# A transformer stack on one core: w_out products behind the next chunk's gate products, norms in parts, modulation vectors on VectorE

## The chip, the cores and the metric

The kernel runs on one core of one Trainium2 chip. The metric is the device time of one execution in microseconds; lower is better. The engines are named as in the profile: PE (TensorE, matrix products), PEld (its weight loads), DVE (VectorE), ACT (ScalarE), POOL (GpSimd) and SP (SyncE, which issues the DMAs).

## The reference

Three blocks follow each other on 512 latent tokens of width 1024, with 256 context tokens beside them in the first layer. Layer 0 is an even mixer (window attention and a gated recurrence) with an FFN, layer 1 an odd mixer (retention) with an FFN, and then a second block (gated delta rule and dilated attention) follows. Each layer computes:

```python
m_lat = jnp.split((cond_lat @ mod_w[layer] + mod_b[layer])[:, None, :], 6, axis=-1)
m_ctx = jnp.split((cond_ctx @ mod_w[layer] + mod_b[layer])[None, None, :], 6, axis=-1)
...
x = x + m_lat[5] * swiglu(modulate(rms_norm(x, norm_g[layer, 1]), m_lat[3], m_lat[4]), ffn_w_in[layer], ffn_w_out[layer])
if not last:
    ctx = ctx + m_ctx[5] * swiglu(modulate(rms_norm(ctx, norm_g[layer, 1]), m_ctx[3], m_ctx[4]), ffn_w_in[layer], ffn_w_out[layer])
...
def swiglu(h, w_in, w_out):
    return (jax.nn.silu(gate) * up) @ w_out    # gate, up = the halves of h @ w_in
```

The FFN is 2816 wide. The second block starts with `mod = silu(c) @ ada_w + ada_b` (3072 columns) and a modulated norm of its own. All is in float32.

## The kernel before

Activations lie transposed: features on the 128 partitions (8 tiles, index k or m_), tokens along the row, 512 for the group `lat` (`xl`, normed copies `hH`, `hL`), 256 for the group `cx` (`xc`, `cH`, `cL`). Every float32 product is made of three PE passes over a high and a low part (`mm3`, lines 140 to 142): wH*xH, wH*xL, wL*xH. Weights come by DMA from SP as 1 MB tiles `wr`; ACT copies the high part `wh` and POOL subtracts the low part `wl` (`wcols`, `wsplit`).

An FFN (`ffn`) runs over 11 chunks of 256 hidden units. In a chunk PE makes, for each group and each half j of the chunk, 24 products for the gate and 24 for the up part; ACT makes the silu, VectorE multiplies (`sg`, line 381) and the result is split again into `aH` (ACT, line 152) and `aL` (VectorE, line 153). Then come the products with w_out, eight output tiles per group of six products each, and VectorE adds each to `xl` or `xc` (`residual`, line 358). The first FFN (f0) has both groups, the second (f1) only `lat`. The PSUM pool `mm` has seven banks there.

A norm (`norm`) sums the squares of the eight tiles (ACT squares into `nt`, VectorE adds into `nacc`, line 339), PE adds over the partitions with a matrix of ones (line 342), ACT makes the reciprocal root (lines 324, 325), and VectorE, ACT and POOL make `hH` and `hL` (lines 348 to 355). Both groups go through it together, and the products behind it start when it is through with the first tiles.

The modulation vectors are matvecs with weights `mod_w` and `ada_w`. They are generators in a list `self.bg`; `tick` advances the first by one 1 MB load. `matvec` multiplies on PE (line 247, tile `mv`), with the loads in side pools `mv1` (8 columns of tiles of layer 1, at the first FFN's norm and behind its end) and `mv2` (12 loads of the second block, around the second FFN). `matvec_dve` multiplies on VectorE (line 277, tile `macc`), and only the sums are handed to PE (line 283); it makes the other vectors of layer 1 in the first FFN.

The order on each engine is fixed when the program is built: a scheduler takes instructions by priority, mostly the order of the code, as their inputs are expected. On the chip each engine runs its list in order.

## Time and profile before

| | us |
|---|---|
| median of 3 runs | 3009.43 (3008.18 to 3015.25) |
| profiled execution | 3007.48 |
| its span, first to last instruction | 3005.4 |
| PE busy | 2810.6 (94%) |
| DVE, ACT, POOL busy | 1372.2, 1053.6, 986.4 |

The mean granted clock of PE over the span is 0.973 of full speed. Busy times of engines overlap, so that they don't add up to the span; where PE is busy, the other engines' work costs no time of its own. The windows of the section on rows cut the span where PE passes from one stage to the next.

### The profile page before, as it was taken

The page shows a single profiled execution, that of the slowest core. Times are in us where ns is not written, and L with a number is a line of the kernel's source. Part 1 is how long each engine was busy: PE and PEld are TensorE (multiplying, and loading weights), DVE is VectorE, ACT ScalarE, POOL GpSimd, SP SyncE. Part 2 cuts the span into 40 slices and gives each one's busy share as a digit, 9 for nine tenths or more (in the row PEclk, how much of TensorE's full clock was granted, in tenths as well). Part 3 has the DMA queues.
Part 4 walks back from the last instruction along what each step waited for, and adds up shares of the span by engine and source line. Part 5 has one row for each costly group of instructions (what it writes and reads, how often), then busy time and mean ns, then how long its engine had stood idle before and what let it go on. Part 6 is the DMA issues. An engine that isn't in the chain of part 4 may idle for free. (4 is left out here: it accounts for less than half of the span.)

```text
span 3005.4 us, 38050 instructions
## 1 busy us (share of the span) xinstructions
PE 2810.6 (94%) x15400; PEld 2288.8 (76%) x15400; DVE 1372.2 (46%) x2218; ACT 1053.6 (35%) x1920; POOL 986.4 (33%) x498
## 2 busy tenths in 40 slices
...
PEclk7999999999999999999999999999999999999999
...
GB/s 263 72 86 82 35 102 69 93 233 98 126 83 142 56 56 71 63 71 70 56 84 56 85 43 168 100 96 98 85 112 156 167 137 87 142 124 108 225 72 89
DMA packets 220824, 312.68 MB, mean 104 GB/s; under 512 B 27430, under 2 KB 172360, under 8 KB 214120
## 3 DMA queue, kind: packets, MB, share of 16 engines
...
## 5 line engine op out<-in xcount | busy, mean ns | idle before, releaser
L134 POOL TENSOR_TENSOR wl<-wr,wh 128x1024 fp32r<-128x1024 f32 x200 | 484.3, 2424 | 921.4 <-ACT wh L133 908.9
L140 PE MATMUL mm<-hH,wh 128*128 128x512 f32 x1760 | 705.8, 402 | 12.9 <-ACT hH L354 7.1
L141 PE MATMUL mm<-hL,wh 128*128 128x512 f32 x1760 | 704.4, 400 | 10.0 <-POOL hL L352 8.9
L142 PE MATMUL mm<-hH,wl 128*128 128x512 f32 x1760 | 700.6, 398 | 0.0
L133 ACT ACTIVATE wh<-wr 128x1024 fp32r<-128x1024 f32 x200 | 211.3, 1058 | 583.1 <-PE mm L141 461.7
L140 PEld LDWEIGHTS mm<-hH,wh 128*128 128x128 f32 x1760 | 334.4, 190 | 94.0 <-ACT hH L354 11.5
L120 POOL TENSOR_TENSOR wl<-wr,wh 128x1024 fp32r<-128x1024 f32 x96 | 236.5, 2466 | 510.1 <-ACT wh L119 484.3
L141 PEld LDWEIGHTS mm<-hL,wh 128*128 128x128 f32 x1760 | 334.2, 190 | 89.8 <-POOL hL L352 13.7
L142 PEld LDWEIGHTS mm<-hH,wl 128*128 128x128 f32 x1760 | 334.4, 190 | 72.8 <-issue 4.4
L358 DVE SCALAR_TENSOR_TENSOR xl<-mm,modT,xl 128x512 f32<-128x512 f32 x216 | 160.4, 749 | 152.1 <-PE mm L142 144.8
L141 PE MATMUL mm<-aL,wh 128*128 128x512 f32 (+1 forms) x528 | 194.9, 369 | 32.9 <-DVE aL L153 32.9
L381 DVE TENSOR_TENSOR sg<-mm,sg 128x512 f32<-128x512 f32 (+1 forms) x66 | 39.7, 601 | 405.0 <-PE mm L142 404.9
L140 PE MATMUL mm<-aH,wh 128*128 128x512 f32 (+1 forms) x528 | 191.1, 367 | 4.0 <-ACT aH L152 4.0
L142 PE MATMUL mm<-aH,wl 128*128 128x512 f32 (+1 forms) x528 | 191.0, 365 | 0.0
L141 PE MATMUL mm<-cL,wh 128*128 128x256 f32 x640 | 184.9, 289 | 0.9 <-POOL cL L352 0.9
L140 PE MATMUL mm<-cH,wh 128*128 128x256 f32 x640 | 183.9, 287 | 1.7 <-ACT rsg L914 1.7
L142 PE MATMUL mm<-cH,wl 128*128 128x256 f32 x640 | 183.7, 287 | 0.0
L119 ACT ACTIVATE wh<-wr 128x1024 fp32r<-128x1024 f32 x96 | 100.9, 1053 | 143.1 <-PE mm L141 83.3
L141 PEld LDWEIGHTS mm<-aL,wh 128*128 128x128 f32 x528 | 102.9, 195 | 55.2 <-DVE aL L153 39.7
L153 DVE TENSOR_TENSOR aL<-sg,aH 128x512 fp32r<-128x512 f32 (+1 forms) x66 | 111.9, 1695 | 44.4 <-ACT aH L152 44.4
L141 PEld LDWEIGHTS mm<-cL,wh 128*128 128x128 f32 x640 | 123.0, 192 | 8.0 <-issue 4.2
L140 PEld LDWEIGHTS mm<-cH,wh 128*128 128x128 f32 x640 | 123.2, 193 | 5.4 <-ACT rsg L914 2.2
...
## 6 DMA issues: line engine op xcount, KB each, us to landing
...
```

The costliest lines, as they stand in the source:

```text
L119: self.nc.scalar.activation(H, rv, AF.Copy)
L120: self.nc.gpsimd.tensor_tensor(L, rv, f32(H), ALU.subtract)
L133: self.nc.scalar.activation(H, v, AF.Copy)
L134: (engs[j] if engs else self.nc.gpsimd).tensor_tensor(L, v, f32(H), ALU.subtract)
L140: mm(out, lH, rH, start=first, stop=False, **kw)
L141: mm(out, lH, rL, start=False, stop=False, **kw)
L142: mm(out, lL, rH, start=False, stop=last, **kw)
L153: (eng or self.nc.gpsimd).tensor_tensor(L, src, f32(H), ALU.subtract)
L358: self.nc.vector.scalar_tensor_tensor(g.x[:, m_, :], po, gate[:, m_:m_ + 1], g.x[:, m_, :], ALU.mult, ALU.add)
L381: nc.vector.tensor_tensor(sg, pu, sg, ALU.mult)
```

## The change

Six things are changed together.

- **FFN in a pipeline.** In chunk c PE makes the gate products, then the w_out products of chunk c-1 (`down`), then the up products. The up weights are loaded apart, `sg` and `aH`/`aL` get buffers for that, and `mm` has eight banks.
- **Norms in parts.** `norm` works on a `Part`: a group, or half of `lat` (256 tokens). Ahead of the FFNs and the odd mixer only the first part is normed; the second part's norm is placed by `between` in the first products (`gemm2`, two weight tiles in turn), and its ones-matmul is put behind the product of k = 3 (`behind`). There `nt` of the first part and the sums `nr` lie in PSUM.
- **Matvecs.** The eight loads of `mod_w` that PE multiplied in layer 1 and the twelve of `ada_w` go to `matvec_dve`, three ticks in each of chunks 1 to 10 of the first FFN (two in chunks 0 to 8 before) and two in chunks 1 to 8 of the second.
- **Ends in parts.** The even mixer's output products run group by group; the odd mixer's last projection and the last w_out products of the second FFN run by halves of 256 tokens.
- **Second block.** Its norm runs by halves with `nt` in PSUM; the transposes of the tokens (`tokens_out`) are no longer deferred.
- The calls of `later`, which deferred ticks, are gone.

The core of the diff (`up` and `gate` are new functions inside `ffn`; `between` is `norm_of(parts[1], mod)`, which calls `norm` with the product to stay behind):

```diff
+    def gemm2(self, pss, ws, part, between=None):
+        for k in range(KT):
+            if between and k == 4:
+                between(last)
+            for ps, (wH, wL) in zip(pss, ws):
+                last = self.mm3(ps[:, part.c], wH[:, k, :], wL[:, k, :], *part.split(k), k == 0, k == KT - 1)
...
+    def matvec_dve(self, ps, sb, i0, n, m, w, c0, bias, dst, tag):
         nc = self.nc
-        m = 2048 // n
         nj = m // 512
+        per = 2048 // m
...
+        for k0 in range(0, KT, per):
+            r = self.wt("wr", [P, per, m])
+            for k in range(per):
                 for i in range(n):
-                    c = self.cond[:, k0 + k, i:i + 1]
+                    c = self.cond[:, k0 + k, i0 + i:i0 + i + 1]
...
+    def norm_stats(self, ps, part, tag="sm", pt=None, after=None):
+        nc, sb, m = self.nc, self.np, part.m
+        acc = self.T(sb, [P, CTX if part.i else LAT], f"nacc{part.i}")[:, :m]
         for k in range(KT):
-            for g, acc in zip(groups, accs):
-                if k == 0:
-                    nc.scalar.activation(acc, g.x[:, k, :], AF.Square)
-                else:
-                    sq = tmp(g)
-                    nc.scalar.activation(sq, g.x[:, k, :], AF.Square)
-                    nc.vector.tensor_tensor(acc, acc, sq, ALU.add)
-        for g, acc in zip(groups, accs):
-            pt = self.T(ps, [P, 512], tag)
-            nc.tensor.matmul(pt[:, :g.m], self.ones, acc, start=True, stop=True)
-            self.rstd(acc, pt[:, :g.m], 1.0 / D)
-        for g, acc, (A, S) in zip(groups, accs, mods):
-            for k in range(KT):
-                t = tmp(g)
-                H, L, s = g.H[:, k, :], g.L[:, k, :], S[:, k:k + 1]
-                nc.vector.scalar_tensor_tensor(t, g.x[:, k, :], A[:, k:k + 1], acc, ALU.mult, ALU.mult)
-                if k % 2:
-                    nc.scalar.activation(t, t, AF.Identity, bias=s)
-                    nc.scalar.activation(H, t, AF.Copy)
-                    nc.gpsimd.tensor_tensor(L, t, f32(H), ALU.subtract)
-                else:
-                    nc.scalar.activation(H, t, AF.Identity, bias=s)
-                    nc.vector.scalar_tensor_tensor(L, t, s, f32(H), ALU.add, ALU.subtract)
-
-    def residual(self, g, m_, po, gate):
-        self.nc.vector.scalar_tensor_tensor(g.x[:, m_, :], po, gate[:, m_:m_ + 1], g.x[:, m_, :], ALU.mult, ALU.add)
+            if k == 0:
+                nc.scalar.activation(acc, part.x(k), AF.Square)
+            else:
+                sq = (self.T(pt[0], [P, 512], "nt", bufs=pt[1]) if pt else self.T(sb, [P, LAT], "nt", bufs=4))[:, :m]
+                nc.scalar.activation(sq, part.x(k), AF.Square)
+                nc.vector.tensor_tensor(acc, acc, sq, ALU.add)
+        r = self.T(ps, [P, 512], tag, bufs=1 if tag == "nr" else None)[:, :m]
+        ins = nc.tensor.matmul(r, self.ones, acc, start=True, stop=True).ins
+        if after:
+            self.behind(ins, after)
+        self.rstd(r, r, 1.0 / D)
+        return r
+    def norm_apply(self, part, r, mod, pt=None):
+        nc, m = self.nc, part.m
+        A, S = mod
+        for k in range(KT):
+            t = (self.T(pt[0], [P, 512], "nt", bufs=pt[1]) if pt else self.T(self.np, [P, LAT], "nt", bufs=4))[:, :m]
+            (H, L), s = part.split(k), S[:, k:k + 1]
+            nc.vector.scalar_tensor_tensor(t, part.x(k), A[:, k:k + 1], r, ALU.mult, ALU.mult)
+            if k % 2:
+                t2 = self.T(self.np, [P, LAT], "nt", bufs=4)[:, :m] if pt else t
+                nc.scalar.activation(t2, t, AF.Identity, bias=s)
+                nc.scalar.activation(H, t2, AF.Copy)
+                nc.gpsimd.tensor_tensor(L, t2, f32(H), ALU.subtract)
+            else:
+                nc.scalar.activation(H, t, AF.Identity, bias=s)
+                nc.vector.scalar_tensor_tensor(L, t, s, f32(H), ALU.add, ALU.subtract)
...
+        def down(wo, hid, order):
+            for m_, p in order:
+                gi = p.g.i
+                po = self.T(ps, [P, 512], "mm")[:, :p.m]
+                for j in range(2):
+                    aH, aL = hid[gi][j]
+                    self.mm3(po, wo[j][0][:, m_ * P:(m_ + 1) * P], wo[j][1][:, m_ * P:(m_ + 1) * P], aH[:, p.c], aL[:, p.c],
+                             j == 0, j == 1)
+                self.residual(p, m_, po, gates[gi])
...
+        for c in range(last + 1):
+            side = lambda i: self.tick(1 if 0 < c < ticks[1] and i < ticks[0] else 0)
+            side(0)
...
+            def up(g, j):
+                pu = self.T(ps, [P, 512], "mm")[:, :g.m]
+                self.gemm(pu, wu[j], g.H, g.L)
+                sg = sgs[g.i][j]
+                nc.vector.tensor_tensor(sg, pu, sg, ALU.mult)
+                aH = self.T(sb, [P, g.m], f"aH{g.i}", F32R, bufs=3 if two else 4)
+                aL = self.T(sb, [P, g.m], f"aL{g.i}", F32R, bufs=3 if two else 4)
+                self.split(sg, aH, aL, nc.vector)
+                hid[g.i][j] = (aH, aL)
...
+            if c == 0:
+                pts = [[self.T(ps, [P, 512], "mm")[:, :g.m] for _ in range(2)] for g in groups[:1]]
+                self.gemm2(pts[0], wg, parts[0], lambda after: between(ps, "mm", after))
+                if not two:
+                    self.gemm2(pts[0], wg, parts[1])
+                for j in range(2):
+                    gate(groups[0], j, pts[0][j])
+                for j in range(2):
+                    up(groups[0], j)
+                if two:
+                    pts = [self.T(ps, [P, 512], "mm")[:, :CTX] for _ in range(2)]
+                    self.gemm2(pts, wg, parts[1])
                     for j in range(2):
-                        aH, aL = hid[j][gi]
-                        self.mm3(po, wo[j][0][:, ms], wo[j][1][:, ms], aH, aL, j == 0, j == 1)
-                    self.residual(g, m_, po, gate)
+                        gate(groups[1], j, pts[j])
+                    for j in range(2):
+                        up(groups[1], j)
+            else:
+                for g in groups:
+                    for j in range(2):
+                        pt = self.T(ps, [P, 512], "mm")[:, :g.m]
+                        self.gemm(pt, wg[j], g.H, g.L)
+                        gate(g, j, pt)
+                side(1)
+                if c < last or two:
+                    down(wdown(c - 1), before, every)
+                side(2)
+                wu = self.wcols(w_in, FFN + c * 256)
+                if c < last:
+                    for g in groups:
+                        for j in range(2):
+                            up(g, j)
+            before, old = hid, before
+        up(groups[0], 0)
+        up(groups[0], 1)
+        if two:
+            up(groups[1], 0)
+            wo = wdown(last)
+            down(wo, hid, [(m_, parts[0]) for m_ in range(KT)])
+            up(groups[1], 1)
+        else:
+            down(wdown(last - 1), old, every)
+            wo = wdown(last)
+            down(wo, hid, [(m_, parts[0]) for m_ in range(KT)])
+        down(wo, hid, [(m_, parts[1]) for m_ in range(KT)])
...
-                mp, ms = side(st, "mv1")
-                matvecs(mp, ms, 1, [2])
-                self.later(30, self.tick, 5)
-                with tc.tile_pool(name="n1ps", bufs=2, space=PSUM, reuse_waits="tile") as ps:
-                    self.norm(ps, groups, mods(0, 1))
+                ms = st.enter_context(tc.tile_pool(name="mv1", bufs=1, reuse_waits="tile"))
+                mod = mods(0, 1)
+                with tc.tile_pool(name="n1ps", bufs=1, space=PSUM, reuse_waits="tile") as ps:
+                    self.norm(ps, parts[0], mod[0], "nr", pt=(ps, 4))
                 with tc.tile_pool(name="f0", bufs=1, reuse_waits="tile") as sb, \
-                        tc.tile_pool(name="f0ps", bufs=7, space=PSUM, reuse_waits="tile") as ps:
-                    for i, m in ((0, 8), (8, 8), (16, 16)):
-                        self.bg.append(self.matvec_dve(ps, ms, 16 // m, a["mod_w"][1], i * P, self.mb[:, 48 + i:48 + i + m],
-                                                       mod1[:, i:i + m, :], "mm"))
-                    self.ffn(ps, sb, groups, gates(mod0, 5), a["ffn_w_in"][0], a["ffn_w_out"][0], (2, 9), pre)
-                    self.tick(99)
+                        tc.tile_pool(name="f0ps", bufs=8, space=PSUM, reuse_waits="tile") as ps:
+                    for i, m, n in ((0, 8, 2), (8, 8, 2), (16, 16, 1), (32, 16, 1)):
+                        self.bg.append(self.matvec_dve(ps, ms, 0, n, m * P, a["mod_w"][1], i * P, self.mb[:, 48 + i:48 + i + m],
+                                                       mod1[:, i:i + m, 0:n], "mm"))
+                    self.ffn(ps, sb, groups, gates(mod0, 5), a["ffn_w_in"][0], a["ffn_w_out"][0], (3, 11), pre, parts,
+                             norm_of(parts[1], mod[1]))
...
+                for i, m in ((0, 16), (16, 8)):
+                    self.bg.append(self.matvec_dve(ps, ms, 2, 1, m * P, a["ada_w_2"][0], i * P, self.mb[:, 96 + i:96 + i + m],
+                                                   self.adaT[:, i:i + m, 0:1], "mm"))
+                self.ffn(ps, sb, [lat], gates(mod1, 5)[:1], a["ffn_w_in"][1], a["ffn_w_out"][1], (2, 9), pre, parts,
+                         norm_of(parts[1], mod))```

What this does to the order, at three places. First PE in the first FFN, where the products for the context group end and the w_out products of chunk 0 begin; `aH_1054` and `aL_1055` are the first half j of the latent group, and `mm` is a PSUM bank. Before:

```order
2741 L140 MATMUL mm_5888<-cH_990_5471,wh_1002_5493 128x256
2742 L141 MATMUL mm_5888<-cL_992_5473,wh_1002_5493 128x256
2743 L142 MATMUL mm_5888<-cH_990_5471,wl_1003_5494 128x256
2744 L140 MATMUL mm_5930<-aH_1054_5745,wh_1072_5922 128x512
2745 L141 MATMUL mm_5930<-aL_1055_5746,wh_1072_5922 128x512
2746 L142 MATMUL mm_5930<-aH_1054_5745,wl_1073_5923 128x512
2747 L140 MATMUL mm_5930<-aH_1059_5802,wh_1074_5926 128x512
2748 L141 MATMUL mm_5930<-aL_1060_5803,wh_1074_5926 128x512
```

These w_out products follow the last up product of the same chunk 0, and the last two `aL` of that chunk, those of the context group, are read three and six rows behind this piece. In the changed program:

```order
2832 L154 MATMUL mm_5974<-cH_990_5471,wh_1070_5889 128x256
2833 L155 MATMUL mm_5974<-cL_992_5473,wh_1070_5889 128x256
2834 L156 MATMUL mm_5974<-cH_990_5471,wl_1071_5890 128x256
2835 L154 MATMUL mm_6017<-aH_1049_5724,wh_1082_6009 128x512
2836 L155 MATMUL mm_6017<-aL_1050_5725,wh_1082_6009 128x512
2837 L156 MATMUL mm_6017<-aH_1049_5724,wl_1083_6010 128x512
2838 L154 MATMUL mm_6017<-aH_1052_5754,wh_1084_6013 128x512
2839 L155 MATMUL mm_6017<-aL_1053_5755,wh_1084_6013 128x512
2840 L156 MATMUL mm_6017<-aH_1052_5754,wl_1085_6014 128x512
```

Here the products ahead are gate products of chunk 1, and the `aH`, `aL` are those of chunk 0; the up products of chunk 1 follow behind the sixteen w_out tiles.

Second ACT at the end of the first FFN and the norm ahead of the odd mixer. Before (`nacc` and `nt` are the squares, line 87 the silu, 152 `aH`):

```order
699 L87 ACTIVATE sg_9881<-mm_9831 128x256
700 L94 ACT_TABLE_LOAD
701 L152 ACTIVATE aH_1606_9884<-sg_9881 128x256
702 L335 ACTIVATE nacc_1648_10082<-xl_5309 128x512
703 L335 ACTIVATE nacc_1649_10083<-xc_5317 128x256
704 L338 ACTIVATE nt_10086<-xl_5309 128x512
705 L338 ACTIVATE nt_10089<-xc_5317 128x256
706 L338 ACTIVATE nt_10092<-xl_5309 128x512
707 L338 ACTIVATE nt_10095<-xc_5317 128x256
```

In the changed program (`wh_1708` is the high part of a tile of the odd mixer's second weight load, line 366 the squares into `nt`):

```order
701 L363 ACTIVATE nacc_1654_10066<-xl_5309 128x512
702 L175 ACTIVATE aH_1629_9968<-sg_1576_9615 128x256
703 L363 ACTIVATE nacc_1682_10182<-xc_5317 128x256
704 L147 ACTIVATE wh_1708_10291<-wr_1707_10289 128x1024
705 L366 ACTIVATE nt_10068<-xl_5309 128x512
706 L366 ACTIVATE nt_10071<-xl_5309 128x512
707 L366 ACTIVATE nt_10074<-xl_5309 128x512
708 L366 ACTIVATE nt_10077<-xl_5309 128x512
709 L366 ACTIVATE nt_10080<-xl_5309 128x512
```

Before, the squares of both groups alternate behind the last `aH`; now a weight copy and then the squares of `lat` alone stand there, and those of the context follow after the steps that make `hH`.

Third POOL at the end of the odd mixer and the norm ahead of the second FFN. Before (`wl_2283` to `wl_2290` are the four tiles of chunk 0):

```order
274 L1007 TENSOR_TENSOR rt_2250_14242<-rt_2250_14242,rsg_14237 128x512
275 L153 TENSOR_TENSOR wl_2268_14350<-wr_2262_14315,wh_2267_14349 128x1024
276 L134 TENSOR_TENSOR wl_2288_14432<-wr_2286_14429,wh_2287_14431 128x1024
277 L134 TENSOR_TENSOR wl_2283_14422<-wr_2281_14419,wh_2282_14421 128x1024
278 L134 TENSOR_TENSOR wl_2285_14426<-wr_2281_14419,wh_2284_14425 128x1024
279 L134 TENSOR_TENSOR wl_2290_14436<-wr_2286_14429,wh_2289_14435 128x1024
280 L352 TENSOR_TENSOR hL_14388<-nt_14477,hH_14386 128x512
281 L352 TENSOR_TENSOR hL_14388<-nt_14486,hH_14386 128x512
```

In the changed program (`wl_2292` to `wl_2299` are the tiles of chunk 0, `wl_2354` is one of chunk 1, `msel` belongs to a matvec):

```order
276 L1122 TENSOR_TENSOR rt_2260_14230<-rt_2260_14230,rsg_14225 128x512
277 L176 TENSOR_TENSOR wl_2276_14310<-wr_2272_14303,wh_2275_14309 128x1024
278 L287 MEMSET msel_14764 128x64
279 L290 MEMSET msel_14764 128x1
280 L148 TENSOR_TENSOR wl_2354_14774<-wr_2352_14771,wh_2353_14773 128x1024
281 L148 TENSOR_TENSOR wl_2292_14443<-wr_2290_14440,wh_2291_14442 128x1024
282 L148 TENSOR_TENSOR wl_2294_14447<-wr_2290_14440,wh_2293_14446 128x1024
283 L148 TENSOR_TENSOR wl_2297_14453<-wr_2295_14450,wh_2296_14452 128x1024
284 L148 TENSOR_TENSOR wl_2299_14457<-wr_2295_14450,wh_2298_14456 128x1024
285 L387 TENSOR_TENSOR hL_14432<-nt_14498,hH_14430 128x256
286 L387 TENSOR_TENSOR hL_14432<-nt_14508,hH_14430 128x256
```

The four splits of chunk 0's weights stand in front of `hL` in both; the split of a tile of chunk 1 has come ahead of them, and the `hL` are 256 columns wide.

## Rows read from the trace of the kernel before

**Rows 1.** The page: busy time by engine, and the slices of PE and its clock.
```profile
PE 2810.6 (94%) x15400; PEld 2288.8 (76%) x15400; DVE 1372.2 (46%) x2218; ACT 1053.6 (35%) x1920; POOL 986.4 (33%) x498
...
PEclk7999999999999999999999999999999999999999
```

**Rows 2.** Waits of PE: line waited for, us in total, times, longest.
```profile
PE mm L141 <- DVE aL L153: 32.9, 21, 1.9
```

**Rows 3.** Windows: length, then busy us of PE, PEld, DVE, ACT, POOL; clock; DMA.
```profile
643.91:725.15 81.24, 65.29 (x333) 48.86 (x334) 68.02 (x77) 30.60 (x53) 29.98 (x15) 0.89 0.50 182
725.15:1263.70 538.55, 520.00 (x2921) 451.35 (x2923) 224.92 (x284) 105.22 (x155) 143.80 (x64) 0.98 0.25 84
1213.10:1263.70 50.60, 50.60 (x294) 44.37 (x296) 21.15 (x36) 16.74 (x29) 11.94 (x5) 1.00 0.22 74
1263.70:1301.67 37.97, 31.20 (x128) 20.62 (x127) 31.90 (x39) 20.13 (x36) 19.35 (x12) 0.91 0.24 82
1827.37:1877.35 49.98, 42.37 (x183) 28.20 (x186) 22.35 (x26) 21.00 (x28) 23.53 (x11) 0.93 0.49 169
1877.35:2227.36 350.01, 336.61 (x1453) 269.34 (x1456) 121.02 (x125) 85.01 (x105) 136.15 (x57) 1.00 0.27 90
2193.96:2227.36 33.40, 33.40 (x149) 26.81 (x151) 11.71 (x17) 10.36 (x15) 7.15 (x3) 1.00 0.18 63
2227.36:2252.92 25.56, 22.38 (x112) 8.68 (x112) 17.46 (x25) 12.96 (x20) 13.42 (x8) 0.93 0.57 191
```

**Rows 4.** Timeline of PE at the first and the third matvec of the first FFN.
```profile
777.60 1.91 PE L283 MATMUL mm<-macc,msel 128*32 128x512 f32 x8
...
780.68 0.50 PE L140 MATMUL mm<-hH,wh 128*128 128x512 f32 x1
...
1104.21 1.06 PE L283 MATMUL mm<-macc,msel 128*32 128x512 f32 x8
...
1106.50 0.48 PE L140 MATMUL mm<-hH,wh 128*128 128x512 f32 x1
```

**Rows 5.** Timeline of PE in a chunk of the second FFN: start, us, gap.
```profile
1904.64 0.51 PE L141 MATMUL mm<-aL,wh 128*128 128x512 f32 x1 [1.49 <-DVE aL L153]
```

**Rows 6.** VectorE multiplies of modulation weights: min/median/max ns.
```profile
L277 DVE SCALAR_TENSOR_TENSOR macc<-wr,cond,macc x35: 1267/1280/4375, 675.5 to 918.0; 128x1024 f32<-128x1024 f32 x28, 128x2048 f32<-128x2048 f32 x7
```

**Rows 7.** Timeline of PE ahead of the first FFN.
```profile
654.09 2.93 PE L342 MATMUL sm<-nacc,ones 128*128 128x512 f32 x4 [6.78 <-DVE nacc L339]
...
659.64 0.73 PE L140 MATMUL mm<-hH,wh 128*128 128x512 f32 x2
```

**Rows 8.** Timeline of VectorE in the same stretch.
```profile
644.35 10.03 DVE L339 TENSOR_TENSOR nacc<-nacc,nt 128x512 f32<-128x512 f32 x12
```

**Rows 9.** Timeline of VectorE at the norm ahead of the odd mixer.
```profile
1265.24 2.78 DVE L339 TENSOR_TENSOR nacc<-nacc,nt 128x512 f32<-128x512 f32 x2 [0.68 <-ACT nt L338]
```

**Rows 10.** ACT groups by form ahead of the first FFN: busy, mean ns | idle.
```profile
L338 ACT ACTIVATE nt<-xl 128x512 f32<-128x512 f32 x4 | 2.5, 626 | 1.6 <-DVE nacc L339 1.6
...
L133 ACT ACTIVATE wh<-wr 128x1024 fp32r<-128x1024 f32 x2 | 2.0, 1049 | 0.1
...
L354 ACT ACTIVATE hH<-nt,modT 128x512 fp32r<-128x512 f32 x1 | 0.7, 722 | 0.5 <-DVE nt L348 0.5
```

**Rows 11.** Timeline of PE at the norm ahead of the second FFN.
```profile
1831.31 1.13 PE L342 MATMUL sm<-nacc,ones 128*128 128x512 f32 x2 [3.94 <-DVE nacc L339]
...
1835.42 2.07 PE L140 MATMUL mm<-hH,wh 128*128 128x512 f32 x4 [1.37 <-ACT hH L354]
```

**Rows 12.** Timeline of PE at the norm ahead of the odd mixer.
```profile
1275.16 0.73 PE L140 MATMUL mm<-hH,wh 128*128 128x512 f32 x2 [2.62 <-ACT hH L354]
```

**Rows 13.** Timeline of POOL at the norm ahead of the second FFN.
```profile
1828.37 5.10 POOL L134 TENSOR_TENSOR wl<-wr,wh 128x1024 fp32r<-128x1024 f32 x2 [3.19 <-ACT wh L133]
1837.29 3.48 POOL L352 TENSOR_TENSOR hL<-nt,hH 128x512 fp32r<-128x512 f32 x2 [3.82 <-ACT hH L351]
```

**Rows 14.** Group by form ahead of the second block: busy, mean ns.
```profile
L247 PE MATMUL mv<-wr,cond 128*32 128x512 f32 x56 | 10.9, 596 | 0.0
```

169 lines of the change are left out of this document (91 added, 78 removed).

## The prediction

> **What bounds the kernel now.** I read the page first: PE is busy for 2810.6 us, 94% of the span, at full clock in 39 of 40 slices, and no other engine passes half of it [rows 1]. So a change is worth what it takes out of PE's idle time, its half-clock time or its instructions. The list of PE's waits comes next: its largest entry is the wait of the w_out products for the last `aL`, 32.9 us in 21 stalls [rows 2], one for each FFN chunk but the last. Third, I cut the span at chunk borders [rows 3]. In the last chunk of the first FFN (1213.10 to 1263.70) PE is busy throughout: 50.6 us is what a chunk costs without a stall; the last chunk of the second FFN gives 33.4 in the same way. Chunks 1 to 10 take 538.55 in the first FFN and 350.0 in the second; what lies above 506.0 and 334.0 can be won there. In the first it is more than the listed waits, because the clock falls after some of them (mean 0.98). The three norms and the start of the second block are windows of their own; there PE is idle for an eighth to a fifth of the time, and the clock is at 0.89 to 0.93.
>
> **1. First FFN, chunks 1 to 10.** Excess 32.55. Part of it is no stall: three matvecs are handed from VectorE to PE, at 3.1 us (777.60 to 780.68), or 2.3 for the one with a single condition (1104.21 to 1106.50) [rows 4]. That is 8.5, so 24.0 are stalls with their clock loss. After the change the w_out products of chunk c-1 stand behind the gate products of chunk c in PE's order, so that their `aL` is made under a third of a chunk of other products, where it was late by a gap of 1.49 [rows 5]. I cost the stall at nothing; its cover is gone only if VectorE falls some 15 us behind. VectorE is busy for 225 of 538 us [rows 3], and gets eight more loads of weights (columns 32 to 48), each one multiply of 128x2048: at 1.28 us for 128x1024 [rows 6], an estimate of 2.6, 21 us in all. That fits. A fourth handover is added, 2.3. New time 506 + 8.5 + 2.3 = 516.8, a gain of 21.8.
>
> **2. Second FFN, chunks 1 to 10.** Excess 16.0, of which ten stalls of 1.49 make 14.9 [rows 5]. They go for the same reason. Two handovers come in, at most 2.3 each. The last w_out products run in halves of 256 columns: by rows 3, 288 products, half of them 256 wide, take 50.6, and 144 of 512 columns take 33.4, so one of 256 costs 0.119 and half of a wide one 0.116; 96 of them lose 0.3. The odd mixer's last projection in halves loses as much. New time 334 + 4.6 + 0.3 = 338.9, a gain of 11.1, less 0.3 in the odd mixer: 10.8.
>
> **3. Norm and chunk 0 of the first FFN.** Now 81.24 from the end of the even block's output products to the end of chunk 0 [rows 3], 30.6 above a free chunk. PE waits 6.78 for the square sums and starts the FFN at 659.64 [rows 7]. VectorE needs 10.03 us for 12 additions, 0.84 each [rows 8]. Now seven additions of one part are enough for a start, which saves up to 5.9. But in the new order ACT's squares come behind two weight copies, and VectorE has nine multiplies of modulation weights between the first addition and the first `nt`, the last three on a load that comes late; nine at 1.28 are 11.5 us. So I put the first product 5 us later than now, 20.8 into the window. At k = 4 PE meets the ones-matmul of the context part, whose sums come behind the first part's work on ACT and VectorE: an estimated 4. With 50.6 of products and 1.6 of half clock that is 77.0, a gain of 4.2, because the stall behind chunk 0's `aL` is gone (bounds: nothing, a gain of 9).
>
> Beside rows 8 and 9 stands a rule. Additions take 0.84 us in one row and 1.39 in the other (2.78 for two): something else decides what they cost. The Trainium skill, "SBUF — State Buffer", section "Who interferes with whom", says that a VectorE instruction with two SBUF inputs and a GpSimd instruction that reads SBUF exclude each other, the later one being blocked to the end, and that one SBUF input makes no such conflict. By this rule additions out of PSUM would be free of POOL's splits: at 0.5 less each, seven in each of four norms, the sum would be 14 us greater; but the 20 new multiplies, with two SBUF inputs, would wait up to 2.5 us each or hold POOL up as long. The longest multiply, 4.4 us where I estimate 2.6 [rows 6], agrees. I keep the sum without it.
>
> **4. Norm ahead of the odd mixer.** Now 37.97 from PE's last w_out product to the end of the q and k products [rows 3], of which 22.3 (two thirds of 33.4) are products. Of the 14 additions two remain at 1265.24 [rows 9]. In the new order ACT's seven squares stand behind a copy of weights that waits for the buffer of the last w_out weights, so none starts before PE is through. The chain from there: copy 1.05, seven squares at 0.63 [rows 10], an addition 0.84, and from the ones-matmul to the first product 4.1 (1831.31 to 1835.42) [rows 11]: 10.4, against 11.46 now [rows 12]. But one part alone is ready then: ACT does twelve steps for it (0.72 each, 8.6) and the context part's eight squares (half as wide, an estimated 0.4 each) before the ones-matmul in PE's order, so k = 4 starts near 21.5, 5.5 after PE gets there. From there 16.7 of products and 1.6 of half clock give 39.8: a loss of 1.8 (bounds 1 gain, 4 loss), although 24 matvec products leave PE.
>
> **5. Norm and chunk 0 of the second FFN.** Now 49.98 [rows 3]; most squares are done when the odd mixer ends, and the first product comes at 1835.42 [rows 11]. In the new program the tiles `nt` share PSUM banks with the mixer's last products, so the squares start after them. In POOL's order five splits of weights stand in front of `hL`, one of them for chunk 1, whose load is issued ahead of chunk 0's; four stood there before, of which two remained (5.10 us, then `hL` at 1837.29) [rows 13]. Four splits from about 1832 end at 1842, and the second k waits for `hL`: some 5 us later than now. With multiplies of 2.6 on VectorE between the additions I take 7.5 on the gate and up products, less 1.6 for the stall behind `aL`: 55.9, a loss of 5.9 (bounds: 2 gain if POOL's order costs nothing, 9 loss).
>
> **6. Start of the second block.** Now 25.56 [rows 3], with 10.9 of matvec products on PE [rows 14]. These go; the norm's chain runs in halves over two PSUM tiles, and twelve more transposes come ahead of its ones-matmul. I take a gain of 2 (bounds 2 loss, 6 gain), since PE's products partly lay under the chain.
>
> **Sum.** 21.8 + 10.8 + 4.2 - 1.8 - 5.9 + 2 = 31.1. The profiled execution took 3007.5, so 2976.4; the median of the runs lies 1.9 higher, which makes 2978. I predict 2977. Terms 1 and 2 may be 3 off together, terms 3 to 6 about 10: 2965 to 2989 for this case.
>
> **Rivals.**
> *The norms overlap as the code is written* (chance 0.16). The first part is ready as its last products end, and the second hides. For it: the parts end one after the other. Against it: the orders of ACT, VectorE and POOL above. The 5 us of term 3, the 5.5 of term 4, the 5 of term 5 and 4 more in term 6 come back: 2957.
> *VectorE's multiplies stall PE* (0.14). The engine works in order; a multiply that waits for its load holds the residuals behind it, and PE fills its eight banks in 8.4 us (six products each, at 0.232 or 0.119). For it: 20 new loads of 1 MB. Against: the gaps left on VectorE. If each load costs PE 1 us, 2997.
> *The other side: weights come late* (0.06). Six loads per chunk share one queue and five buffers; a modulation load that takes a buffer ahead of the up weights delays products that now have them early. For it: the up weights are loaded apart and late. Against: five buffers in a chunk of 50 us. The change is slower from 1.6 us in each of 20 chunks on; at 2.5 us it gives 3027.
> *The change does not do what it says* (0.06): PE waits as long as now, because VectorE runs that far behind. Terms 1 and 2 turn to -7, the time is near 3016; half of the stalls back give 2997. Against it: 225 of 538.
> *My case*: 0.58.
>
> **How the numbers follow.** The measurement tells changes from about 0.3% (9 us) on, so faster means below 3000. My case, the first rival and most of the second lie there, with half of the last: 0.87; slower 0.07, between them 0.06. A range of 2954 to 2999 holds my case, most of the first two rivals, and leaves out the other two and the tails.
>
> **What would show it.** Right: no row of PE's waits for `aL` in the FFNs; chunks of 50.6 and 33.4 but for handovers; windows of 517 and 339; norm windows of 40 and 56, with PE waiting for the second part's `nacc` and for `hL`. Wrong: longer chunks with PE waiting for `wl`, residuals or loads; norm windows far from 40 and 56. Most likely to make it wrong are terms 3 to 6, estimated from an order.

## The result and the profile after

The changed kernel takes 2981.09 us in the median of four runs (2980.38 to 2982.47), against 3012.34 for the kernel before, timed beside it on the same chip: a ratio of 0.9892, with a 95% interval of 0.9866 to 0.9918. The forecast was 2977, in a range of 2954 to 2999. The time lies 4 us off the forecast; two of its terms are off by more than that, both to the worse, and terms that came out better, with a gain that was not in the sum, make up for most of it. The mechanism of the two largest terms was right; that the number came so near is in part luck.

The page of the changed kernel, busy times and the clock in 40 slices, which answer to [rows 1]:

```profile
span 2978.9 us, 38262 instructions
...
PE 2778.8 (93%) x15432; PEld 2296.7 (77%) x15432; DVE 1397.7 (47%) x2291; ACT 1059.8 (36%) x1964; POOL 993.0 (33%) x512
...
PEclk7999999989999999899999998999999999999999
```

PE is busy 31.8 us less. The clock row has three slices at 8 where before had none: these are the three norms.

The list of PE's waits of the changed kernel (line waited for, us in total, times, longest):

```profile
PE nr L369 <- DVE nacc L367: 32.4, 5, 17.9
PE mm L154 <- DVE hL L390: 23.1, 3, 9.4
...
PE mm L155 <- POOL hL L387: 6.3, 5, 2.3
```

The wait for `aL` that headed the list before [rows 2] has gone from it. In its place stand two waits of the norms, together 55.5 us. The first, for the sums, was 11.7 us before:

```profile
PE sm L342 <- DVE nacc L339: 11.7, 3, 6.8
```

The second is new and strange: the first product of a norm (line 154, which reads `hH` and `wh`) waits for an `hL` that it doesn't read, three times.

Windows of the changed kernel (length, busy us of PE, PEld, DVE, ACT, POOL, granted clock, DMA): the norm and chunk 0 of the first FFN, its other chunks, its last 288 products, the norm ahead of the odd mixer, the norm and chunk 0 of the second FFN, its other chunks, and its last 192 products, half of them 256 wide. They answer to [rows 3]; where before closed a chunk with its w_out products, PE has now made the next chunk's gate products, which take as long (16.8 us in the first FFN, 11.1 in the second).

```profile
639.10:721.80 82.70, 55.38 (x293) 47.10 (x293) 51.01 (x64) 35.23 (x62) 27.06 (x16) 0.81 0.36 125
721.80:1237.25 515.45, 512.25 (x2930) 445.12 (x2928) 240.43 (x298) 98.74 (x138) 146.22 (x66) 1.00 0.29 99
1186.96:1237.25 50.29, 50.29 (x286) 43.72 (x284) 25.37 (x40) 6.22 (x9) 7.69 (x4) 1.00 0.26 88
1237.25:1281.47 44.22, 27.80 (x101) 20.82 (x100) 32.39 (x45) 26.19 (x51) 18.66 (x13) 0.77 0.15 48
1805.55:1859.90 54.35, 39.79 (x197) 34.54 (x198) 41.56 (x51) 28.10 (x55) 34.81 (x17) 0.84 0.62 215
1859.90:2196.39 336.49, 334.89 (x1509) 273.72 (x1507) 143.00 (x149) 82.50 (x101) 141.92 (x60) 1.00 0.30 97
2163.10:2196.39 33.29, 33.29 (x192) 29.16 (x190) 18.65 (x27) 7.67 (x11) 9.60 (x4) 1.00 0.20 60
```

So the two FFNs run as a row of products at full clock (0.98 before in the first), with no gap but the 0.8 us at each handover of a matvec, and the three norm windows run at 0.77 to 0.84 (0.89 to 0.93 before), with PE idle for a third of the first and of the second. Stage by stage, the span of the two profiles is made up so:

| stage, us | before | after | difference |
|---|---|---|---|
| up to the last output product of the even block | 643.91 | 639.10 | -4.8 |
| norm 1 and chunk 0 of the first FFN | 81.24 | 82.70 | +1.5 |
| its other chunks | 538.55 | 515.45 | -23.1 |
| norm 2, to the first product of the context part | 39.74 | 44.22 | +4.5 |
| odd mixer | 523.96 | 524.07 | +0.1 |
| norm 3 and chunk 0 of the second FFN | 49.98 | 54.35 | +4.4 |
| its other chunks | 350.01 | 336.49 | -13.5 |
| the rest, to PE's last product | 769.34 | 773.84 | +4.5 |
| behind PE's last product | 8.68 | 8.70 | 0.0 |

The sum is -26.5, the difference of the spans (3005.4 and 2978.9).

Where the norms lose is seen on PE and VectorE. First PE's timeline of the changed kernel at norms 1, 2 and 3 (start, us, in brackets the gap ahead and what ended it), which answers to [rows 7, 11, 12]:

```profile
657.01 2.07 PE L369 MATMUL nr<-nacc,ones 128*128 128x512 f32 x2 [17.91 <-DVE nacc L367]
668.50 0.79 PE L154 MATMUL mm<-hH,wh 128*128 128x512 f32 x1 [9.41 <-DVE hL L390]
...
1244.58 2.08 PE L369 MATMUL nr<-nacc,ones 128*128 128x512 f32 x2 [7.32 <-DVE nacc L367]
1254.84 0.80 PE L154 MATMUL mm<-hH,wh 128*128 128x512 f32 x1 [8.19 <-DVE hL L390]
...
1809.60 0.70 PE L369 MATMUL nr<-nacc,ones 128*128 128x256 f32 x2 [4.06 <-DVE nacc L367]
1815.79 0.58 PE L154 MATMUL mm<-hH,wh 128*128 128x256 f32 x1 [5.49 <-DVE hL L390]
```

From the ones-matmul to the first product it is 11.5, 10.3 and 6.2 us, where it was 4.1 to 5.6 before. VectorE in norm 1 of the changed kernel, which answers to [rows 8]:

```profile
641.24 1.87 DVE L298 TENSOR_SCALAR macc<-wr,cond 128x1024 f32<-128x1024 f32 x1 [2.02 <-DMA wr<-in_mod_w_dram]
...
656.88 4.86 DVE L300 SCALAR_TENSOR_TENSOR macc<-wr,cond,macc 128x1024 f32<-128x1024 f32 x4
661.66 2.06 DVE L382 SCALAR_TENSOR_TENSOR nt<-xl,nA,nr 128x512 f32<-128x512 f32 x3
663.64 0.74 DVE L390 SCALAR_TENSOR_TENSOR hL<-nt,modT,hH 128x512 fp32r<-128x512 f32 x1
...
667.70 0.75 DVE L390 SCALAR_TENSOR_TENSOR hL<-nt,modT,hH 128x512 fp32r<-128x512 f32 x1
```

The first `hL` is there at 664.4, but the product starts at 668.50, right behind the third (for k = 4) at 667.70. Ahead of the first `nt`, multiplies of modulation weights hold VectorE.

### The profile page after: what moved, and what is told of

The parts are those of the page before. It is cut to its first block, busy times and chain, and to the rows that moved or that the text cites. A ratio compares the mean times of both kernels' runs of the same rounds, so it can differ in the third digit from the quotient of the medians.

```text
span 2978.9 us, 38262 instructions
## 1 busy us (share of the span) xinstructions
PE 2778.8 (93%) x15432; PEld 2296.7 (77%) x15432; DVE 1397.7 (47%) x2291; ACT 1059.8 (36%) x1964; POOL 993.0 (33%) x512
## 3 DMA queue, kind: packets, MB, share of 16 engines
q8 instruction: 121, 1.98, 0.3%
## 5 line engine op out<-in xcount | busy, mean ns | idle before, releaser
L148 POOL TENSOR_TENSOR wl<-wr,wh 128x1024 fp32r<-128x1024 f32 x200 | 485.9, 2431 | 1005.2 <-ACT wh L147 978.4
L154 PE MATMUL mm<-hH,wh 128*128 128x512 f32 (+1 forms) x1776 | 713.1, 402 | 32.1 <-DVE hL L390 23.1
L155 PE MATMUL mm<-hL,wh 128*128 128x512 f32 (+1 forms) x1776 | 708.1, 399 | 6.5 <-POOL hL L387 6.0
L156 PE MATMUL mm<-hH,wl 128*128 128x512 f32 (+1 forms) x1776 | 704.9, 397 | 0.0
L154 PEld LDWEIGHTS mm<-hH,wh 128*128 128x128 f32 x1776 | 340.0, 192 | 111.4 <-DVE hL L390 26.6
L147 ACT ACTIVATE wh<-wr 128x1024 fp32r<-128x1024 f32 x200 | 211.4, 1059 | 553.0 <-PE mm L155 446.4
L155 PEld LDWEIGHTS mm<-hL,wh 128*128 128x128 f32 x1776 | 340.2, 192 | 80.0 <-POOL hL L387 7.4
L156 PEld LDWEIGHTS mm<-hH,wl 128*128 128x128 f32 x1776 | 340.2, 192 | 71.2 <-issue 3.9
L134 POOL TENSOR_TENSOR wl<-wr,wh 128x1024 fp32r<-128x1024 f32 x96 | 239.3, 2496 | 399.8 <-ACT wh L133 399.8
L400 DVE SCALAR_TENSOR_TENSOR xl<-mm,modT,xl 128x512 f32<-128x512 f32 (+1 forms) x228 | 163.3, 721 | 283.8 <-PE mm L156 276.7
L154 PE MATMUL mm<-aH,wh 128*128 128x512 f32 (+1 forms) x544 | 191.0, 352 | 0.0
L156 PE MATMUL mm<-aH,wl 128*128 128x512 f32 (+1 forms) x544 | 190.7, 351 | 0.0
L155 PE MATMUL mm<-aL,wh 128*128 128x512 f32 (+1 forms) x544 | 190.5, 350 | 0.0
L154 PE MATMUL mm<-cH,wh 128*128 128x256 f32 x640 | 184.1, 288 | 3.7 <-DVE nt L382 2.9
L155 PE MATMUL mm<-cL,wh 128*128 128x256 f32 x640 | 184.5, 288 | 0.0
L156 PE MATMUL mm<-cH,wl 128*128 128x256 f32 x640 | 183.5, 287 | 0.0
L133 ACT ACTIVATE wh<-wr 128x1024 fp32r<-128x1024 f32 x96 | 101.1, 1054 | 171.6 <-PE mm L155 103.5
L154 PEld LDWEIGHTS mm<-cH,wh 128*128 128x128 f32 x640 | 123.3, 193 | 7.8 <-DVE nt L382 3.3
L155 PEld LDWEIGHTS mm<-cL,wh 128*128 128x128 f32 x640 | 123.3, 193 | 6.7 <-issue 4.2
L176 DVE TENSOR_TENSOR aL<-sg,aH 128x512 fp32r<-128x512 f32 (+1 forms) x66 | 107.9, 1634 | 39.8 <-ACT aH L175 39.8
L156 PEld LDWEIGHTS mm<-cH,wl 128*128 128x128 f32 x640 | 123.3, 193 | 2.8 <-issue 2.5
L300 DVE SCALAR_TENSOR_TENSOR macc<-wr,cond,macc 128x1024 f32<-128x1024 f32 (+1 forms) x56 | 105.0, 1890 | 20.5 <-DMA wr<-in_mod_w_dram 14.4
```

The costliest lines, as they stand in the source:

```text
L133: self.nc.scalar.activation(H, rv, AF.Copy)
L134: self.nc.gpsimd.tensor_tensor(L, rv, f32(H), ALU.subtract)
L147: self.nc.scalar.activation(H, v, AF.Copy)
L148: (engs[j] if engs else self.nc.gpsimd).tensor_tensor(L, v, f32(H), ALU.subtract)
L154: mm(out, lH, rH, start=first, stop=False, **kw)
L155: mm(out, lH, rL, start=False, stop=False, **kw)
```

## The experiments

**Theories.** A: two things that hang on placement delay the norms. The first is the PSUM banks: a tile that a norm's engines still read lies in the bank of the first product, which so waits for the last of these reads. In the changed program the tile `nt` for k = 4 lies in PSUM bank 0, and the first product's tile `mm` is given bank 0 too. The second is the matvecs, whose first loads and multiplies are scheduled into norm 1. B: the parts themselves cost; norming a part first and the other between the products makes PE wait in the middle, wherever tiles lie.

All runs, by stage as in the table above: h is the first product behind the norm's start, w the first w_out product (in before and p2_nopipe, chunk 1's gate products of 16.8 and 11.1 us come behind w, in all others ahead of it), c the first context product; the rest ends with PE's last product. The stages are those of one profiled execution of each kernel.

| kernel | norm 1 h, w | norm 2 h, c | odd mixer | norm 3 h, w | rest | median | ratio, interval |
|---|---|---|---|---|---|---|---|
| before | 15.7, 54.0 | 11.5, 39.7 | 524.0 | 8.0, 36.8 | 769.3 | 3012.3 | |
| after | 29.4, 82.7 | 17.6, 44.2 | 524.1 | 10.2, 54.4 | 773.8 | 2981.1 | 0.9892, 0.9866 to 0.9918 |
| e1_bank | 23.8, 84.4 | 12.0, 37.3 | 528.4 | 5.4, 55.5 | 773.3 | 2981.1 | 0.9897, 0.9880 to 0.9914 |
| e2_late | 18.3, 70.6 | 17.3, 43.6 | 524.1 | 10.3, 54.5 | 776.9 | 2970.0 | 0.9855, 0.9841 to 0.9870 |
| e3_both | 13.0, 71.8 | 12.3, 38.5 | 529.3 | 5.7, 50.6 | 774.9 | 2964.5 | 0.9841, 0.9824 to 0.9858 |
| e4_sbuf | 23.4, 77.6 | 11.3, 36.9 | 524.4 | 5.9, 55.7 | 778.5 | 2973.6 | 0.9869, 0.9855 to 0.9884 |
| e5_sbuf_late | 22.0, 74.9 | 10.4, 36.9 | 524.2 | 5.9, 53.8 | 777.8 | 2965.1 | 0.9840, 0.9825 to 0.9855 |
| p1_whole | 22.9, 74.5 | 13.4, 43.3 | 523.7 | 22.6, 57.8 | 777.5 | 2976.2 | 0.9879, 0.9865 to 0.9894 |
| p2_nopipe | 27.2, 63.7 | 17.3, 43.5 | 524.3 | 12.0, 46.4 | 772.9 | 3035.9 | 1.0075, 1.0060 to 1.0090 |
| p3_nomv | 29.4, 82.7 | 17.3, 43.7 | 524.3 | 10.3, 53.9 | 773.7 | 2970.4 | 0.9864, 0.9849 to 0.9879 |
| p4_whole_late | 20.2, 73.2 | 13.9, 44.2 | 523.8 | 20.8, 56.9 | 769.0 | 2961.7 | 0.9827, 0.9810 to 0.9843 |
| p6_whole_late_sums | 14.7, 67.2 | 6.9, 35.0 | 524.5 | 8.5, 55.8 | 769.3 | 2957.6 | 0.9824, 0.9803 to 0.9846 |
| p7_sbuf_late_sums | 14.6, 70.9 | 4.8, 43.8 | 523.8 | 6.3, 54.0 | 773.7 | 2967.9 | 0.9856, 0.9842 to 0.9871 |
| p8_mixed | 14.8, 67.2 | 6.9, 34.9 | 524.4 | 9.0, 55.4 | 765.3 | 2951.5 | 0.9807, 0.9783 to 0.9832 |

The kernel before had medians of 3012.6 to 3014.4 beside these runs.

**The banks.** A padding tile in two norm pools, and another order of the odd mixer's pools, put the first product in a bank that no `nt` has had:

```diff
+nc.scalar.activation(self.T(ps, [P, 512], "pad")[:, :1], self.eps, AF.Square)   # n1ps, n3ps
...
-tc.tile_pool(name="odmm", ...), tc.tile_pool(name="odsm", ...), tc.tile_pool(name="odo", ...)
+tc.tile_pool(name="odo", ...), tc.tile_pool(name="odsm", ...), tc.tile_pool(name="odmm", ...)
```

> The changed kernel, with the PSUM banks of the first gate and query products moved away from those of the norm's tiles nt (a bank is set aside in the pools of the norms ahead of the FFNs, and the odd mixer's pools are opened in another order). Theory A, the first product after a norm waits for its PSUM bank, which an nt tile of k = 4 still holds: PE's first product comes 4 us earlier in the norms ahead of the first FFN and the odd mixer and 2 us ahead of the second FFN, and the time falls by 7 to 10 us, to about 2972. Rival B, the product waits for the low parts hL as a whole or for VectorE's pace: the gaps stay at 9.4, 8.2 and 5.5 us and the time stays within 2 us of 2981.

The first products come 5.6, 5.6 and 4.9 us earlier, and their wait for `hL` is gone. That is the bank; nothing else ahead of them was changed. The total stays, though. In norms 1 and 3 PE's next wait takes its place, for the second part's sums (5.8 us in norm 3; norm 1 in this row of PE's timeline of that kernel). Norm 2 keeps 6.9 us, but the odd mixer takes 4.3 us more under its new order of pools.

```profile
673.65 1.22 PE L369 MATMUL mm<-nacc,ones 128*128 128x256 f32 x2 [4.18 <-DVE nacc L367]
```

**The matvecs begun later.** The ticks begin at chunk 3 of the first FFN (two at a chunk's start to make up) and at chunk 2 of the second:

```diff
-side = lambda i: self.tick(1 if 0 < c < ticks[1] and i < ticks[0] else 0)
+side = lambda i: self.tick((2 if two and i == 0 and c < 8 else 1) if (2 if two else 1) < c < ticks[1] and i < ticks[0] else 0)
...
-self.ffn(..., (2, 9), pre, parts,    # second FFN
+self.ffn(..., (2, 10), pre, parts,
```

> The changed kernel, with VectorE's matvecs starting two chunks later in the first FFN and one chunk later in the second, so that in VectorE's order no multiply stands between the additions and the first nt of the norm ahead of the first FFN. Theory A, these multiplies (nine of 1.27 us, one waiting for its load) make the first product late: the ones-matmul comes some 8 us and the first product 10 to 13 us earlier, and the time falls by 9 to 13 us, to about 2970. Rival B, ACT's weight copies in front of the squares or the clock set the start: under 3 us. If the loads pressed together in the later chunks hold up the weights, PE waits for wl there and the time rises.

Norm 1 is 12.1 us shorter, the other norms and the odd mixer are within 0.7 us of what they were (the rest is 3 us longer), and the time falls by 11 us. VectorE's row of that kernel shows the seven additions in one piece, with nothing between:

```profile
640.81 5.44 DVE L367 TENSOR_TENSOR nacc<-nacc,nt 128x512 f32<-128x512 f32 x7 [1.98 <-ACT nt L366]
```

Both edits together:

> Both edits of the two runs before together. If the two causes are apart, the gains add up: 16 to 23 us, about 2961. If one hides behind the other (the bank is free by the time that the late norm is through), the gain is that of the larger alone, about 11 us, near 2970.

By the medians another 5.6 us, which the intervals don't tell from nothing. In norm 1 the first product comes 5.2 us earlier than with the late matvecs alone, and the first w_out product no earlier (71.8 against 70.6). Norm 2 gains 5.1 us, which the odd mixer gives back (529.3 against 524.1), and norm 3 gains 3.9; the last experiment shows whether that is a gain.

**`nt` in SBUF.** The squares and `nt` of the three first parts go back to SBUF, so that no `nt` holds a bank (`"nr", pt=(ps, 4)` becomes `"nr"`), with the ticks as in the changed kernel, and then late:

> The changed kernel with the tiles nt of the three first-part norms back in SBUF (four buffers, as before the change); the sums nr stay in PSUM. Theory A, PSUM tiles cost more than they save: the waits for banks go (4, 4 and 2 us), and in the norm ahead of the odd mixer the squares no longer wait for PE's last product, 3 to 5 us more; the time falls by about 10, to 2971. Rival B, additions with two SBUF inputs are blocked by POOL's weight splits: each addition beside a split grows from 0.68 to 1 us or more, the norm ahead of the first FFN gets 3 us longer, and the sum is between -5 and +5 us.

> The changed kernel with both edits of two earlier runs, nt of the first parts in SBUF and VectorE's matvecs later. Theory A, the two act on different norms (SBUF on the one ahead of the odd mixer, 7 us; the later matvecs on the one ahead of the first FFN, 12): 2962 to 2965. If in the first norm the bank wait and the multiplies are in one chain, that norm gains no more than 12 together. Rival B, additions from SBUF are blocked by POOL's splits once the multiplies are gone: the norm ahead of the first FFN is 3 us or more longer than with nt in PSUM, and the time is 2967 to 2970.

Norm 2 gains 7.3 us, and norm 1 gains 5.1. With late ticks norm 1 is 4.2 us longer than with `nt` in PSUM (74.9 against 70.6), and the first product still comes 10.6 us behind its ones-matmul (11.43, the second of its two passes, to 22.00), though no `nt` lies in PSUM. What holds it, and why the sums are later, is found below.

**Without the pipeline.** The w_out products stand in their own chunk again; all else is as changed:

```diff
-if c < last or two:
-    down(wdown(c - 1), before, every)
...
+down(wdown(c), hid, every)   # behind the chunk's up products
```

> The changed kernel with the other part undone: the w_out products of a chunk stand behind the up products of the same chunk again, as before the change; eight banks, norms and matvecs stay changed. Theory A, the stalls for aL come back in each chunk, 24 us in the first FFN with their half clock, 10 in its chunk 0 and 15 in the second: 40 to 50 us more, 3020 to 3030, slower than the kernel before. Rival B, the stalls had another cause or the eighth bank and the separate loads of the up weights make part of the gain: under 30 us more.

The kernel takes 54.8 us more than the changed one and 0.75% more than the one before. In PE's list of waits the old entry is back:

```profile
PE mm L155 <- DVE aL L176: 30.9, 19, 3.5
```

So the pipeline is worth all of the gain and more, and the rest of the change by itself is a loss, a larger one than was expected. The second FFN takes 372.2 us from its first w_out product, 9 more than before; two handovers of matvecs are 4.5 of that, and a wait of 3.9 us for an `aH`, which before doesn't have, is most of the rest. That the new multiplies on VectorE made this `aH` late, and that the pipeline hides it, is likely but not shown.

**Without the 20 loads.** Only the bias is copied where their sums would go, so this kernel leaves a part of the modulation vectors out.

```diff
-for i, m, n in ((0, 8, 2), (8, 8, 2), (16, 16, 1), (32, 16, 1)):
+nc.scalar.activation(mod1[:, 32:48, 0], self.mb[:, 80:96], AF.Copy)
+for i, m, n in ((0, 8, 2), (8, 8, 2), (16, 16, 1)):
...
-self.bg.append(self.matvec_dve(ps, ms, 2, 1, m * P, a["ada_w_2"][0], ...))
+nc.scalar.activation(self.adaT[:, 0:24, 0], self.mb[:, 96:120], AF.Copy)
```

> The changed kernel without the 20 added loads of modulation weights: in the place of what they give (the two last sixths of the second block's modulation for the FFN, and three of another) only the bias is copied, so their products are left out. Theory A (VectorE's multiplications delay norms 1 and 3, and little else): norm 1 up to the first product of w_out takes 12 us less, as with the loads begun a chunk later, FFN 1 up to 3 us less, and the second block loses no loads: 2965 to 2971 us. Theory B (the loads and VectorE's work beside the FFN chunks cost as well, by their DMA queue and the handovers to TensorE): FFN 0 and FFN 1 run faster in their chunks too, by 0.5 us in each of ten and more, 2955 to 2964 us.

Both theories missed the place. Norm 1 doesn't move (82.7): what stands in it are the first loads, of columns 0 to 16, which VectorE multiplied before as well, but from 675.5 on, in chunk 0 [rows 6]. The chunks of the FFNs get shorter, by 2.7 and 5.0 us, near the handovers that go (one of 2.3, two of 2.3 and 2.2). The time falls by 10.7; the two profiles differ by 7.5, of which the FFNs are 7.7.

**Norms in one piece.** All of a norm ahead of its products, as before the change, in the order sums, then multiplications, with `nt` in SBUF and `between` empty:

```diff
+def norm_whole(self, ps, parts, mods):
+    rs = [self.norm_stats(ps, p) for p in parts]
+    for p, r, mod in zip(parts, rs, mods):
+        self.norm_apply(p, r, mod)
...
-self.norm(ps, parts[0], mod[0], "nr", pt=(ps, 4))
+self.norm_whole(ps, parts, mod)
```

> The changed kernel with one part undone: ahead of the two FFNs and the odd mixer the norm again takes all its tokens in one piece, with nt in SBUF, and nothing is put between the first products; the FFN pipeline, the matvecs and the second block stay changed. Theory A, the norms in parts are a net loss there, by 11.9, 4.5 and 6.5 us in the traces: the time falls by 12 to 22 us, to 2960 to 2969, the less the more multiplies still stand in VectorE's first norm. Rival B, the norm in one piece would suffer as much from the multiplies and from POOL's splits as the parts do, and the losses come from the matvecs on VectorE alone: the time stays within 5 us of 2981.

> The FFN pipeline and the matvecs on VectorE with all norms in one piece (those of the first run of this set and the second block's too, with its transposes deferred again), and VectorE's matvecs later. If the norms in parts lose 23 us in all against the kernel before, as the traces say, this is the best of the kernels so far: 2953 to 2960. If a part of that loss belongs to the FFN's eight banks or to the loads (whole norms start no earlier than 15 us after PE's last product), 2960 to 2966.

The first is 5 us faster than the changed kernel by the medians, where 12 to 22 were expected; norm 1 is 8.2 us shorter, norm 3 is 3.4 longer. The second (late ticks, and the second block's norm in one piece with its transposes deferred again) was the fastest up to then. But its norms are slow: 20.8 us to the first product of norm 3, where before took 8.0. PE's timeline of that kernel at norms 1 and 3, and VectorE's at norm 1, between them:

```profile
659.46 0.76 PE L154 MATMUL mm<-hH,wh 128*128 128x512 f32 x1 [4.89 <-DVE nt L382]
...
1816.62 0.58 PE L154 MATMUL mm<-hH,wh 128*128 128x256 f32 x1 [16.25 <-DVE nt L382]
```
```profile
657.91 1.40 DVE L382 SCALAR_TENSOR_TENSOR nt<-xl,nA,sm 128x512 f32<-128x512 f32 x2
```

The first product waits for an `nt` again, and for the last one: the two multiplications that end at 659.31 are k = 6 and 7. They read the tile `sm`, and that is the bank. The changed code leaves the reciprocal root in the PSUM tile of the ones-matmul, from which all eight multiplications read; before, it went to `nacc` in SBUF and the bank was free at once. The pools give the tile of the sums and the first `mm` tile bank 0 both. One edit undoes it:

```diff
-        self.rstd(r, r, 1.0 / D)
-        return r
+        self.rstd(acc, r, 1.0 / D)
+        return acc
```

> The changed kernel with all norms in one piece, the late matvecs and the second block's norm in one piece (the kernel that took 2961.67 us), and with one thing more: the result of the reciprocal root goes back into the SBUF tile of the sums, as in the kernel before, where the change leaves it in the PSUM tile of the ones-matmul, from which all eight multiplications by it read. Theory A (the PSUM tile of the sums holds its bank until the last of these multiplications, and the first product's tile lies in that bank): the first product comes as soon as the first split is there, about 5.6 us behind the ones-matmul as before (7.7 + 5.6 = 13.3 us into the window of norm 1 in place of 20.2; some 8 in place of 20.8 for norm 3), and what follows comes earlier too, though the last splits still pace it: 5 us for norm 1, 5 for norm 2, 8 for norm 3, 2944 us in all, between 2938 and 2953. Theory B (the splits alone set the pace: what comes first only waits later, as with the two banks that were padded before): the first products come early, the first product of w_out does not, 2959 to 2963 us.

> The norms in parts as in the changed kernel, with their squares in SBUF and the late matvecs (the kernel that took 2965.07 us), and with the reciprocal root's result back in SBUF. The first product's tile lies in the bank of the sums here as well, and it came 22.0 us into the window of norm 1 and 5.9 us into that of norm 3. Theory A: the first product of norm 1 comes some 6 us earlier, but the second part's norm still comes between k = 3 and k = 4, so that no more than 3 us of it are kept: 2959 to 2964 us, and the whole norms with the same edit are faster than the parts by 10 us or more. Theory B: 2964 to 2967 us, and the whole norms stay within 5 us of the parts.

In the whole norms the first product comes 5.5, 7.0 and 12.3 us earlier. In norms 1 and 2 it is kept (6.0 and 9.3 us), in norm 3 only 1.1 of it. By the profiles the span falls from 2966.8 to 2953.6, but the first of these is the slowest of its four runs; by the medians it is 4 us, which the intervals don't tell from nothing. What is shown is the stages. The expectation's theory A is right in norms 1 and 2 and wrong in norm 3, where the splits set the pace as its theory B had it. In the parts the first product comes 7.4 us earlier in norm 1, and the sum doesn't change: its norm 2 ends 7 us later than without the edit; PE waits 8.1 us there for `rsg`, ACT's copy of the q and k products, where it waited 0.7:

```profile
1256.97 0.79 PE L154 MATMUL mm<-hH,wh 128*128 128x512 f32 x1 [8.08 <-ACT rsg L1018]
```

On ACT the context part's steps stand ahead of that copy. The whole norms lead by 10 us in the medians and 13 in the profiles: 3.7 are norm 1, 8.9 norm 2 and 4.4 the rest, where the second block's norm differs too; norm 3 is 1.9 longer. So in norms 1 and 2 the charge of this section's theory B against the parts holds too.

What is left in norm 3 is seen in the whole norm of the faster kernel (`p6_whole_late_sums`), on POOL and on VectorE:

```profile
1790.66 10.92 POOL L148 TENSOR_TENSOR wl<-wr,wh 128x1024 fp32r<-128x1024 f32 x4 [20.61 <-ACT wh L147]
1801.54 1.74 POOL L387 TENSOR_TENSOR hL<-nt,hH 128x512 fp32r<-128x512 f32 x1
```
```profile
653.56 0.74 DVE L382 SCALAR_TENSOR_TENSOR nt<-xl,nA,nacc 128x512 f32<-128x512 f32 x1
...
1791.00 5.61 DVE L382 SCALAR_TENSOR_TENSOR nt<-xl,nA,nacc 128x512 f32<-128x512 f32 x2
1796.54 2.83 DVE L390 SCALAR_TENSOR_TENSOR hL<-nt,modT,hH 128x512 fp32r<-128x512 f32 x1
```

Four splits of weights stand in POOL's order ahead of its first `hL`. While they run, a multiplication and an `hL` take VectorE 2.8 us each, as long as a split; in norm 1, at 653.56, when POOL was through, a multiplication takes 0.74. `p4_whole_late`, which differs by that one edit, shows the other side, POOL and VectorE in its norm 3, where the multiplications, of the same size, read the root from PSUM:

```profile
1802.72 10.20 POOL L148 TENSOR_TENSOR wl<-wr,wh 128x1024 fp32r<-128x1024 f32 x4 [20.43 <-ACT wh L147]
```
```profile
1801.71 2.72 DVE L382 SCALAR_TENSOR_TENSOR nt<-xl,nA,sm 128x512 f32<-128x512 f32 x4 [3.47 <-ACT sm L349]
...
1808.43 0.75 DVE L382 SCALAR_TENSOR_TENSOR nt<-xl,nA,sm 128x512 f32<-128x512 f32 x1
```

With one operand in PSUM they take 0.75 each beside the splits, unhindered. The additions of norm 1 show the same. In `e5_sbuf_late` three of the seven, from SBUF, run beside POOL's splits at 2.5 to 2.6 us each:

```profile
641.39 7.84 POOL L148 TENSOR_TENSOR wl<-wr,wh 128x1024 fp32r<-128x1024 f32 x3 [12.47 <-ACT wh L147]
```
```profile
641.79 7.99 DVE L367 TENSOR_TENSOR nacc<-nacc,nt 128x512 f32<-128x512 f32 x3
```

In `e2_late` all seven, from PSUM, took 5.44 us beside splits as well, so that the ones-matmul came 8.0 us into the norm there and 10.4 here. The rule that the Trainium skill states on "SBUF — State Buffer", section "Who interferes with whom" (two SBUF inputs on VectorE and a GpSimd read exclude each other, one SBUF input doesn't), agrees with these rows. So the PSUM tiles of the change buy something, and pay for it with the bank. And the root that went back to SBUF freed a bank in norm 3 but made its readers wait for the splits.

**Each norm in the form that was best.** Norms 1 and 2 and the second block's whole with the root in SBUF, norm 3 in parts with `nt` and root in PSUM and a padding tile:

> The whole norms with the late matvecs and the reciprocal root back in SBUF (the kernel that took 2957.62 us), but with the norm ahead of FFN 1 in two parts, as in the kernel with a padded bank and late matvecs, where the first product of w_out came 50.60 us behind the odd mixer's end, against 55.80 us with that norm whole. All else stays. Theory A (for this norm the parts are better, since POOL's splits of weights stand ahead of those of the norm, and the first half hides them; each norm's form can be chosen by itself): 50.6 us there again, 5 us less in all, 2949 to 2956 us. Theory B (what one stage gains, a neighbour gives back, the odd mixer above all, which took 528 to 529 us in place of 524 in the kernels whose banks were padded): 2956 to 2961 us.

It is the fastest kernel of the study, 2951.53 us, and its interval lies below that of the changed kernel; from `p6_whole_late_sums` its runs don't separate it. Its total lies in the range of theory A, but the expectation failed in the place: norm 3 takes 55.4, not 50.6. The 50.6 us of `e3_both` had been paid for in the odd mixer: odd mixer and norm 3 together take 579.9 there and 579.8 here. From the profile of `p6_whole_late_sums` to this one there are 5.9 us: 4.0 lie behind the second FFN and 1.4 ahead of norm 1, where nothing was changed.

## Why the prediction was right, and where not

**Terms 1 and 2 were right.** The first FFN's chunks take 515.45 us (forecast 516.8), the second's 336.49 (338.9); PE has no wait for `aL` in either. A chunk costs 50.29 and 33.29, and the matvecs' handovers cost what was said, as PE's timeline shows at the third of them in the first FFN, from 1030.39 to 1032.68, which answers to [rows 4]:

```profile
1030.39 1.06 PE L307 MATMUL mm<-macc,msel 128*32 128x512 f32 x8
1032.27 0.66 PE L316 MATMUL mm<-ident,mrow 128*128 128x128 f32 x4 [0.81 <-DVE mrow L309]
1032.68 0.48 PE L154 MATMUL mm<-aH,wh 128*128 128x512 f32 x1
```

VectorE's work was hidden, at 240 of 515 us. Without the pipeline the gain is lost and 0.75% more, so that these two terms carry the result.

**Term 3 was mis-sized**, a loss of 1.5 in place of a gain of 4.2. Its step was the first product at 20.8 us; it came at 29.4. The 20.8 was made of the start of before, 11.5 us for the nine multiplies, and up to 5.9 saved on additions that a start no longer needs. The multiplies were sized right: with late ticks the first product comes 11.1 us earlier. What failed is the saving. Without the multiplies the first product came at 18.3, not ahead of the 15.7 of before; 5.2 us of that are the bank, which the prediction didn't have, and with the bank free as well (`e3_both`, 13.0) the saving is 2.7. The 4 us at k = 4 were hidden behind the late first product; with the bank free they are there (4.18 us in `e1_bank`).

**Term 4 was mis-sized**: 4.5 lost, not 1.8. The chain was put at 10.4 us up to the first product; the ones-matmul came at 7.3, but the product at 17.6, because of the bank. With a free bank (`e1_bank`) it came at 12.0 and the stage took 37.3, a gain of 2.4. The wait of 5.5 us at k = 4 was in neither. (The forecast's window ended with the q and k products; to there it is 43.5 after 37.97, a loss of 5.5.)

**Term 5 was nearly right in size**, 4.4 lost of a forecast 5.9, and in its reason: POOL's four splits stand ahead of `hL`, whose first came at 1818.16. ACT and POOL in norm 3 of the changed kernel:

```profile
1807.80 1.99 ACT L147 ACTIVATE wh<-wr 128x1024 fp32r<-128x1024 f32 x2
```
```profile
1808.92 9.29 POOL L148 TENSOR_TENSOR wl<-wr,wh 128x1024 fp32r<-128x1024 f32 x4 [8.44 <-ACT wh L147]
1818.16 6.02 POOL L387 TENSOR_TENSOR hL<-nt,hH 128x256 fp32r<-128x256 f32 x4
```

One step further back stands ACT: POOL had been idle for 8.44 us, and ACT's first copies of these weights, at 1807.80, stand behind all seven squares in its order, where before two of the four splits were made by the odd mixer's end. With the bank free, PE's first product of norm 3 waits for such a copy (4.93 us in `e1_bank`). No run moved these copies. No variant won here: odd mixer and norm 3, up to the first w_out product, took 571.8 us before (with the 11.1 of gate products) and 577.7 in the best of them. The bank had a part in it too, but `e1_bank` and `e3_both` show that it brings nothing alone.

**Term 6 missed its gain.** The rest takes 4.5 us longer, where 2 were to be gained, but little of the loss lies at the start of the second block. PE's transposes of `baT`, which follow its first products, come 168.4 us behind the second FFN before and 168.9 in the changed kernel; in `p6_whole_late_sums`, with that norm whole, 162.9. PE's timelines of the three:

```profile
2395.73 0.42 PE L1082 MATMUL mm<-ident,baT 16*128 16x16 f32 x4
```
```profile
2365.33 0.42 PE L1199 MATMUL mm<-ident,baT 16*128 16x16 f32 x4
```
```profile
2338.86 0.42 PE L1202 MATMUL mm<-ident,baT 16*128 16x16 f32 x4
```

With the norm in halves all kernels lie at 168.1 to 169.6 there, with it whole (p4, p6, p8) at 161.2 to 162.9. So the gain was to be had, and the halves, or the transposes that were no longer deferred, cost it; those two were not tried apart. The other 4 us come later, where the code is that of before: from `baT` to PE's last product it is 600.9 us before and 602.4 to 608.9 in all kernels of the study. What makes that vary is open.

**Outside the sum**, 4.8 us were won ahead of norm 1. In the other kernels, unchanged there, that stretch ends between 637.3 and 641.7 us, so some 4 us of it vary by themselves. No run took this apart.

Of the rivals, "the norms overlap as the code is written" is what the banks, the early ticks and the splits prevent. "VectorE's multiplies stall PE" was right in one place only, norm 1; without the 20 loads the FFNs gain little more than the handovers. Late weights were not seen in the chunks, and that PE waits as long as now is ruled out by its list of waits. The rule that the prediction set beside rows 8 and 9 and left out of the sum holds here, as the norms' additions show; of the 14 us that it might have added, the tiles in PSUM give 4 in norm 1 (`e2_late` against `e5_sbuf_late`), and the bank takes 7 in norm 2.
